# A hybrid SSD / MLA / stick-breaking trunk: sums and transfers around the FFN moved in the program, padded k_pe for the scores, one product of two k-tiles moved

## The chip, the cores and the metric

The kernel runs on one core of a Trainium2 chip. The metric is the device time of one execution in microseconds; lower is better. Times given for a kernel are the median of several runs, and beside them stands one execution under the hardware profiler, whose trace all readings of the profile use.

TensorE (PE in the profile) multiplies matrices, VectorE (DVE) and ScalarE (ACT) work elementwise, GpSimd (POOL) and SyncE (SP) here mostly issue transfers.

## The reference

A trunk of two pre-norm residual layers over 256 positions of width 2048, float32. Layer 0 runs a Mamba-2 mixer and latent attention (MLA) side by side behind one input projection and into one output projection. Layer 1 is stick-breaking attention. Each layer is followed by a SwiGLU FFN with a hidden width of 5632:

```python
def swiglu_ffn(h, w_gate, w_up, w_down):
    return (jax.nn.silu(h @ w_gate) * (h @ w_up)) @ w_down

# MLA, 16 heads, two query blocks of 128 (q_nope, k_nope: 128 wide; q_pe, k_pe: 64 wide, k_pe shared)
s = (jnp.einsum('bqhd,bkhd->bhqk', q_nope[:, q0:q1], k_nope[:, :q1])
     + jnp.einsum('bqhr,bkr->bhqk', q_pe[:, q0:q1], k_pe[:, :q1])).astype(jnp.float32) * scale

for layer in range(DEPTH):
    h = rms_norm(x, mix_norm[layer])
    ...
    x = x + mix
    x = x + swiglu_ffn(rms_norm(x, ffn_norm[layer]), w_gate[layer], w_up[layer], w_down[layer])
return rms_norm(x, final_norm)
```

## The kernel before

**Numbers.** Products are kept near float32 by splitting each operand into a high part (fp32r) and the rest. ScalarE casts the high part (`split`, L316), VectorE subtracts it (L322), and a product of one k-tile (128 rows of the contraction) is three matmuls: high by high, low by high, high by low. Activations are split once, each weight tile (128 x 4 k-tiles x 512, 1 MB) once as it is used.

**Weight tiles.** `weight_slots` lays out an arena: three slots for high parts (`wh`, a fourth from the first output projection on), six (`w`) into which SP loads raw tiles and in which the low part takes the raw tile's place, two (`wsum`) for sums of weight tiles. `wtile` gives out the free slot that was last used longest ago. The residual x lives in `xres`, behind the slots. During an FFN, from its second pair on, `lend` turns `xres` into one more `w` and one more `wsum` slot ("lent" in the profile); x waits in DRAM meanwhile (`saved`, four blocks of 512 columns, 512 KB each), where the partial results of the down projection are added by transfers. `load_residual` brings it back at the FFN's end.

**Pairs.** Two projections of the same operand (512 columns each, left and right) are one `pair`. For two groups of four k-tiles it uses seven products of a Strassen-like scheme (M1 to M7, 12 matmuls each) instead of eight, with four accumulators in PSUM (z, p3, p2, p4); some products need sums of weight tiles (t1, t2, M3's and M4's, `wsub`, L673), and accumulators that two results share are copied out in between (`kept`, L747, ScalarE). The order is written out as a list. In HALF the other eight k-tiles are four tiles c0 to c3 of plain products (24 matmuls each), 180 matmuls in all. In MORE the k-tiles 8 to 11 go through seven half-size products as well (n0, n1, n2, n3, six matmuls a product, with half-size sums t1 to t4), 174 in all. In "n0" the split tile serves M1 and then M2; "n2" serves M5 and then M6 from the sum T2. MORE needs sums of the activation blocks, made by `more_sums`; the FFN uses HALF for its first two pairs and MORE from the third (n >= 2).

**FFN.** Eleven pairs of gate and up, each giving 512 columns of h (`left` and `right`, L846 to L852). h is rounded by a transfer in SBUF that POOL issues (L855, the "h words") and transposed on TensorE (L327) in a task, `wait` ticks into the next work. Every second pair's h goes into four `down` projections (48 matmuls each), of which two follow each later pair; the last three chunks go into the final projections (72 matmuls each).

**Order.** TensorE's instructions run in the order of the text. Tasks (`spawn`) are generators that are advanced a step when the number of ticks that they yielded has gone by; there is a tick about every six matmuls. On the other engines a list scheduler orders the instructions by data and by rank (`priority`, `urgent`); `issue_after` puts an instruction behind another one on its engine. `s2` tiles come from a pool of 42.

**Start of an FFN.** While the second pair of the output projection before it runs, `norm_next` prepares the FFN's operand: blocks 0 and 1 through `norm_operand`, blocks 2 and 3 through `norm_block` (transposes, L329; split with the gain, L347 and L349; square sums, L312). Each writes its block of xres to `saved` (L536, L465). `more_sums` (L505 on) follows block 2.

**Scores.** `mla_head` adds three matmuls per query block into one tile: nope (L1417), rope (L1418, over 64 partitions: k_pe stands twice, in each half of `kpeT`, and a head uses the half in which its q_pe lies) and the mask (L1419, bf16).

Of the kernel before, what the change touches and what calls it, by code (L numbers as in the profile page):

```python
# [15 lines left out]
P = 128  # L16
# [24 lines left out]
class Trunk:  # L41
# [204 lines left out]
    def constant_tiles(self, rows_m, rows_a, rows_b):  # L246
        nc = self.nc
        c = lambda shape, name, dt=F32: self.cp.tile(shape, dt, name=name)
        self.ident = c([P, P], "ident")
        make_identity(nc, self.ident)  # L250
        warm = self.small([P, 1], "warm")
        nc.scalar.activation(warm, self.ident[:, 0:1], AF.Exp)
        self.ident_r = c([P, P], "ident_r", F32R)
        nc.gpsimd.dma_start(self.ident_r.bitcast(F32), self.ident)
        self.identb = c([P, P], "identb", BF16)
        make_identity(nc, self.identb)
        self.ones = c([P, P], "ones")
        nc.gpsimd.memset(self.ones, 1.0)

        self.tri_u = c([P, P], "tri_u")  # L260
        nc.gpsimd.affine_select(self.tri_u, self.ones, [[1, P]], ALU.is_ge, 0.0, base=0, channel_multiplier=-1)
        tri_l = self.s2([P])
        nc.gpsimd.affine_select(tri_l, self.ones, [[-1, P]], ALU.is_ge, 0.0, base=0, channel_multiplier=1)
        self.tri_l, self.ones_r = c([P, P], "tri_l", F32R), c([P, P], "ones_r", F32R)
        nc.gpsimd.tensor_copy(self.tri_l, tri_l)
        nc.gpsimd.tensor_copy(self.ones_r, self.ones)
        zero = self.s2([P])
        nc.gpsimd.memset(zero, 0.0)

        self.cmask = c([P, P], "cmask", BF16)  # L270
        nc.gpsimd.affine_select(self.cmask, zero, [[-1, P]], ALU.is_ge, NEG, base=0, channel_multiplier=1)

        self.vm, self.va, self.vb = c([P, 32], "vm"), c([P, 56], "va"), c([P, 120], "vb")
        self.g_mix = (self.vm[:, 0:16], self.vm[:, 16:32])
        self.g_ffn = (self.va[:, 0:16], self.va[:, 16:32])
# [55 lines left out]
    def transpose_split(self, src, res, g=None, wait=3, rank=None):  # L331

        for k2 in range(2):
            yield wait if k2 == 0 else 1
            pt = self.tr([2, S])
            for k in range(2):
                for t in range(2):
                    self.transpose(pt[:, k, t * P:(t + 1) * P], src(t, 2 * k2 + k))
            hi, lo = self.s2([2, S], F32R), self.s2([2, S], F32R)
            if g is None:  # L340
                with self.urgent() if rank == self.URGENT else self.priority(rank or self.tc.cur_priority):
                    self.split(hi, lo, pt)
            else:
                with self.urgent() if rank == self.URGENT else self.priority(rank or self.tc.cur_priority):
                    gk = [g[:, kk:kk + 1] for kk in (2 * k2, 2 * k2 + 1)]
                    for k in range(2):
                        act = self.nc.scalar.activation(hi[:, k], pt[:, k], AF.Copy, scale=gk[k])  # L347
                    for k in range(2):
                        dve = self.nc.vector.scalar_tensor_tensor(lo[:, k], pt[:, k], gk[k], hi[:, k].bitcast(F32),  # L349
                                                                  op0=ALU.mult, op1=ALU.subtract)  # L350
                if rank and rank >= 99000 and k2 == 0:
                    self.first = [act.ins, dve.ins]
            res.append((hi, lo))
# [101 lines left out]
    def norm_block(self, st, j, g, wait=2, rank=None, blocks=False, spill=None, pause=2):  # L455

        x, res = self.xres, []

        def gen():
            yield from self.transpose_split(  # L460
                lambda t, k: x[:, t, j * 512 + k * P:j * 512 + (k + 1) * P], res, g[:, 4 * j:4 * j + 4], wait, rank)
            for t in range(2):
                self.square_sum(x[:, t, j * 512:(j + 1) * 512], st["ssq"][:, t, j:j + 1])
            if spill is not None:
                self.nc.gpsimd.dma_start(spill[j], x[:, :, j * 512:(j + 1) * 512])  # L465
        st["xT"].append((self.spawn(gen()), res))
        if blocks and j == 1:
            self.make_sums(st, pause)
# [36 lines left out]
    def more_sums(self, st):  # L505

        sub = lambda o, p, q: self.nc.vector.tensor_tensor(o, p, q, op=ALU.subtract)
        add = lambda o, p, q: self.nc.vector.tensor_tensor(o, p, q, op=ALU.add)
        yield 1
        self.join(st["xT"][2][0])  # L510
        a = {}
        for j, (hi, lo) in enumerate(st["xT"][2][1]):
# [16 lines left out]
    def norm_operand(self, st, j, g):  # L529

        x = self.xres

        def squares():
            for t in range(2):
                self.square_sum(x[:, t, j * 512:(j + 1) * 512], st["ssq"][:, t, j:j + 1])
            self.nc.gpsimd.dma_start(self.saved[j], x[:, :, j * 512:(j + 1) * 512])  # L536
        self.operand_block(st, j, lambda t, k: x[:, t, j * 512 + k * P:j * 512 + (k + 1) * P],
                           g[:, 4 * j:4 * j + 4], squares, 9)

# [125 lines left out]
        w.left = uses  # L665
        return wh, wl, w

    def wsub(self, o, p, q, so=None, sp=None, sq=None):

        half = lambda w, n: w.raw if n is None else w.raw[:, 2 * n:2 * n + 2]  # L670
        with self.priority(self.wprio):
            self.wprio += 100
            ins = self.nc.vector.tensor_tensor(half(o, so), half(p, sp), half(q, sq), op=ALU.subtract).ins  # L673
        for w in (p, q):
            w.readers.append(ins)
        if not o.readers:
            self.filled(o, ins)
# [4 lines left out]

    MORE = ("M1", "M5", "c2", "t1", "t2", "t4", "n0", "n2", "M3", "M6", "M2", "t3", "M4", "n1", "M7", "n3", "c3")

    LATE = ("M1", "M5", "M3", "M6", "M2", "M7", "M4", "c0", "c1", "c2", "c3")

    def pair(self, st, va, vb, left, right, order=HALF):

# [79 lines left out]

        def halves(w, *ms):
            wh, wl, slot = w
            for n, (m, keep) in enumerate(ms):
                at = slice(2 * n, 2 * n + 2)
                add(bank[m], more_ops(m), (wh[:, at], wl[:, at], slot), keep and m)
        for m in order:
# [12 lines left out]
                self.wsub(src["n3"], raw["c0"], src["n2"], 0, 1, 1)  # L791
                continue
            if m == "n0":
                halves(self.wsplit(raw["c0"], 4, 4, mybir.DependencyClass.Sync), ("M1", True), ("M2", False))
                continue
            if m == "n2":
                halves(self.wsplit(src["n2"], 4, 4, mybir.DependencyClass.Sync), ("M5", True), ("M6", False))
# [11 lines left out]
            if m == "M5":  # L809
                self.wsub(t2, b22, t1)  # L810
            if m == "M3":
                self.wsub(b12, b22, b12)
            if m == "M6":
                load("b21")
                b21 = src["M2"] = raw["b21"]
# [6 lines left out]
            if m[0] == "c":  # L822
# [3 lines left out]
                    add(b, x[b in ("z", "p4")], w)  # L826
                continue
            add(bank[m], ops(m), w, m if m in keeps else None)

    def lend(self):  # L830

# [4 lines left out]
    def ffn(self, layer, st, gain_next):  # L836
# [308 lines left out]
    def dt_and_krope(self, rstd, xT):  # L1145
# [260 lines left out]
    def mla_head(self, h, qp, q, k, v, g, o, wait, done):  # L1406
# [6 lines left out]
        pr = slice(64 * (h % 2), 64 * (h % 2) + 64)  # L1413
        sc = self.at([3 * P])
        for q0, q1, c0, ks in ((0, P, 0, P), (P, S, P, S)):
            dst = sc[:, c0:c0 + ks]
            nc.tensor.matmul(dst, qT[:, q0:q1], kT[:, 0:ks], start=True, stop=False)  # L1417
            nc.tensor.matmul(dst, qpT[pr, q0:q1], self.kpeT[pr, 0:ks], start=False, stop=False)  # L1418
            nc.tensor.matmul(dst[:, ks - P:ks], self.identb, self.cmask, start=False, stop=True)  # L1419
        mx, sm = self.small([P, 2], "mx"), self.small([P, 2], "sm")  # L1420
        p = self.s2([3 * P])
# [74 lines left out]
```

## Time and profile before

| | |
|---|---|
| median of 3 runs | 2420.68 us (2420.16 to 2421.95) |
| profiled execution | 2423.95 us, span 2422.2 us, mean granted TensorE clock 0.996 |
| TensorE busy | 2382.6 us (98%), 10936 matmuls |
| VectorE busy | 2007.2 us (83%) |
| ScalarE busy | 1463.6 us (60%) |
| transfers | 497.88 MB, mean 206 GB/s |
| first MLA scores, last | 428.9 us, 560.9 us |
| first FFN pair of layer 0 | from about 634 us |
| steady FFN stretch of layer 0 | a pair and two downs every 62.4 us |

The span is the time from the first to the last instruction of the profiled execution; times below are from its start. Busy times of matmuls overlap, so the distance from one start to the next is the better measure of a product's cost.

### The profile page before, as it was taken

How to read it: one execution, taken by the hardware profiler on the slowest of the kernel's cores; microseconds unless marked ns; L12 is line 12 of the kernel's file. 1: busy time of each engine (PE TensorE's matmuls, PEld its weight loads, DVE VectorE, ACT ScalarE, POOL GpSimd, SP SyncE). 2: the span in 40 equal slices, each digit the busy share in tenths (PEclk: the TensorE clock that was granted, in tenths of full speed). 3: DMA queues.
4: the chain of work that ended last, by engine and by line, in shares of the span. 5: the costliest groups of instructions: out<-in, count | busy, mean ns of one | idle time of the engine just before them, and what ended most of it. 6: DMA issues, size and time to landing. Idle time of an engine off the chain costs nothing.

```text
span 2422.2 us, 28061 instructions
## 1 busy us (share of the span) xinstructions
PE 2382.6 (98%) x10936; PEld 1956.7 (81%) x10936; DVE 2007.2 (83%) x1664; ACT 1463.6 (60%) x1480; POOL 233.8 (10%) x301
## 2 busy tenths in 40 slices
PE   8999999999999999999999999999999999999998
PEld 7888888777778888888888888888778888888877
DVE  6776597578999888888887989779998888998874
ACT  6665465555755665656655686775655565666663
POOL 1342001120000000000010010000000000000011
PEclk9999999999999999999999999999999999999999
DMA  7655556434656777777776555556667777777773
GB/s 261 201 182 192 186 191 186 117 131 156 222 196 226 221 232 230 220 233 235 224 222 225 199 175 180 184 174 226 211 206 229 224 226 224 227 226 229 226 251 119
DMA packets 274902, 497.88 MB, mean 206 GB/s; under 512 B 22924, under 2 KB 48144, under 8 KB 274768
## 3 DMA queue, kind: packets, MB, share of 16 engines
q1 hardware_dynamic: 255440, 446.48, 55.7%
q0 software_dynamic: 18752, 48.55, 8.0%
q8 instruction: 86, 1.41, 0.2%
q10 hardware_dynamic: 576, 1.05, 0.1%
q14 instruction: 48, 0.39, 0.0%
HBM read 459.24 MB, written 25.20 MB: 200 GB/s over the span
## 4 chain that ended last, share of the span: by engine, by line
PE 73%; issue 13%; DVE 9%; DMA 2%; POOL 2%; ACT 1%; SPq 0%; POOLq 0%; DVEq 0%; ACTq 0%
PE acc L726 39%; PE acc L421 10%; PE acc L424 10%; PE acc L423 10%; DVE wsum L673 2%; DVE wsum L322 2%; DVE w L322 2%; DMA s<-s 1%; DVE lent L322 1%; DVE lent L673 1%; PE at L1341 1%; PE tr L327 1%; DVE w L673 0%; POOL s L1245 0%; DVE s L322 0%
## 5 line engine op out<-in xcount | busy, mean ns | idle before, releaser
L322 DVE TENSOR_TENSOR w<-w,wh 128x2048 fp32r<-128x2048 f32 (+2 forms) x397 | 885.8, 2242 | 199.4 <-ACT wh L316 189.4
L726 PE MATMUL acc<-wh,s 128*128 128x512 f32 x3888 | 991.6, 393 | 7.3 <-DVE s L322 3.1
L316 ACT CAST wh<-w 128x2048 fp32r<-128x2048 f32 (+2 forms) x397 | 741.6, 1874 | 350.1 <-PE acc L424 133.8
L726 PEld LDWEIGHTS acc<-wh,s 128*128 128x128 f32 x3888 | 727.4, 189 | 160.1 <-ACT s L747 4.3
L421 PE MATMUL acc<-wh,s 128*128 128x512 f32 (+1 forms) x1280 | 510.8, 399 | 2.0 <-ACT wh L316 2.0
L424 PE MATMUL acc<-wh,s 128*128 128x512 f32 (+1 forms) x1280 | 496.9, 388 | 0.0
L423 PE MATMUL acc<-w,s 128*128 128x512 f32 (+1 forms) x1200 | 464.9, 387 | 0.0
L726 PE MATMUL acc<-w,s 128*128 128x512 f32 x1304 | 355.7, 391 | 0.4 <-DVE w L322 0.4
L726 PEld LDWEIGHTS acc<-w,s 128*128 128x128 f32 x1304 | 245.7, 189 | 53.5 <-DVE w L322 1.8
L424 PEld LDWEIGHTS acc<-wh,s 128*128 128x128 f32 x1280 | 240.8, 188 | 50.3
L421 PEld LDWEIGHTS acc<-wh,s 128*128 128x128 f32 x1280 | 241.2, 188 | 48.0 <-ACT wh L316 2.4
L423 PEld LDWEIGHTS acc<-w,s 128*128 128x128 f32 x1200 | 226.3, 189 | 43.6 <-issue 1.4
L316 ACT CAST wh<-wsum 128x2048 fp32r<-128x2048 f32 x103 | 186.7, 1813 | 74.7 <-DVE wsum L673 53.3
L322 DVE TENSOR_TENSOR wsum<-wsum,wh 128x2048 fp32r<-128x2048 f32 x103 | 222.8, 2163 | 4.0 <-ACT wh L316 4.0
L316 ACT CAST wh<-lent 128x2048 fp32r<-128x2048 f32 (+1 forms) x66 | 120.5, 1836 | 75.4 <-DMA lent<-in_w_gate_dram 33.6
L322 DVE TENSOR_TENSOR lent<-lent,wh 128x2048 fp32r<-128x2048 f32 (+1 forms) x66 | 144.0, 2186 | 8.6 <-ACT wh L316 8.2
L673 DVE TENSOR_TENSOR wsum<-w,wsum 128x2048 f32<-128x2048 f32 (+1 forms) x52 | 106.1, 2041 | 25.0 <-PE acc L726 20.9
L726 PE MATMUL acc<-wsum,s 128*128 128x512 f32 x388 | 109.2, 396 | 5.9 <-DVE wsum L322 5.3
L747 ACT COPY s<-acc 128x512 f32<-128x512 f32 x132 | 77.0, 584 | 57.2 <-PE acc L726 57.0
L855 POOL DMA_DIRECT2D s<-s x44 | 24.5, 557 | 783.7 <-DVE s L852 733.9
L726 PEld LDWEIGHTS acc<-wsum,s 128*128 128x128 f32 x388 | 72.1, 189 | 26.3 <-DVE wsum L322 11.8
L871 POOL DMA_DIRECT2D saved<-s x64 | 56.5, 1026 | 331.1 <-ACT s L870 331.1
(262 smaller groups left out, 1868.6 us busy)
## 6 DMA issues: line engine op xcount, KB each, us to landing
w<-in_w_down_dram SPq DMA_DIRECT2D x78, 1024.0 KB, 5.0
w<-in_w_gate_dram SPq DMA_DIRECT2D x76, 1024.0 KB, 5.1
w<-in_w_up_dram SPq DMA_DIRECT2D x76, 1024.0 KB, 5.2
w<-in_w_qkv_dram SPq DMA_DIRECT2D x48, 1024.0 KB, 5.0
w<-in_w_in_dram SPq DMA_DIRECT2D x47, 1024.0 KB, 5.1
w<-in_w_out_even_dram SPq DMA_DIRECT2D x32, 1024.0 KB, 5.0
saved<-s POOLq DMA_DIRECT2D x64, 256.0 KB, 6.7
w<-in_w_out_odd_dram SPq DMA_DIRECT2D x16, 1024.0 KB, 4.9
```

Of the source, the lines that this page charges most:

```text
L316: cast = nc.scalar.copy(hi, src).ins
L322: return nc.vector.tensor_tensor(lo, src, hi.bitcast(F32), op=ALU.subtract).ins
L327: self.nc.tensor.transpose(out.bitcast(F32R), src, self.ident_r)
L421: nc.tensor.matmul(ps[t], hi[:, ts], wh, start=k == 0, stop=False)
L423: slot.used(nc.tensor.matmul(ps[t], hi[:, ts], wl, start=False, stop=False), self.clock)
L424: nc.tensor.matmul(ps[t], lo[:, ts], wh, start=False, stop=k == nk - 1)
L673: ins = self.nc.vector.tensor_tensor(half(o, so), half(p, sp), half(q, sq), op=ALU.subtract).ins
L726: m = nc.tensor.matmul(ps[b], x, y, start=b not in started, stop=stop, skip_group_check=True)
L747: self.kept = nc.scalar.copy(o, ps[b]).ins
L855: nc.gpsimd.dma_start(words.bitcast(F32), h[t])
L871: nc.gpsimd.dma_start(self.saved[n][:, t], s, accum_op=ALU.add)
L1341: nc.tensor.matmul(py[:, ds], rows[c, h // 4][:, h % 4], xdt[c][:, ds], start=True, stop=True)
```

## The change

- `more_sums` begins 40 ticks after it is spawned instead of one; MORE begins with the fourth pair (n >= 3).
- The four writes of xres to `saved` leave `norm_operand` and `norm_block` (as called ahead of an FFN) and become a task at the FFN's start, one each four ticks. It is joined before `lend`.
- The four reads of `saved` at the FFN's end become a task, the first after 12 ticks, then one each six.
- h's transposes wait ten ticks instead of six, except the last chunk's.
- In the first pair, M3's weight sum is queued on VectorE behind the low part of operand block 2.
- In MORE, the M2 part of n0 becomes an entry of its own, n4, behind n2.
- `kpeT` becomes two tiles of 128 partitions, each with k_pe in one half and zeros in the other; the rope product runs over 128 partitions. The tile of ones becomes a view of `ones_r`.

```diff
@@ constant_tiles
-        self.ones = c([P, P], "ones")
-        nc.gpsimd.memset(self.ones, 1.0)
+        ones = self.s2([P])
+        nc.gpsimd.memset(ones, 1.0)
...
-        nc.gpsimd.tensor_copy(self.ones_r, self.ones)
+        nc.gpsimd.tensor_copy(self.ones_r, ones)
+        self.ones = self.ones_r.bitcast(F32)
@@ transpose_split
+                self.lo = dve.ins
@@ norm_block
+            if j == 2:
+                st["lo"] = self.lo
@@ more_sums
-        yield 1
+        yield 40
         self.join(st["xT"][2][0])
@@ norm_operand
-            self.nc.gpsimd.dma_start(self.saved[j], x[:, :, j * 512:(j + 1) * 512])
@@ wsub
-        with self.priority(self.wprio):
+        with self.priority(self.wprio), self.tc.issue_after(after) if after else nullcontext():
@@
-    MORE = ("M1", "M5", "c2", "t1", "t2", "t4", "n0", "n2", "M3", "M6", "M2", "t3", "M4", "n1", "M7", "n3", "c3")
+    MORE = ("M1", "M5", "c2", "t1", "t2", "t4", "n0", "n2", "n4", "M3", "M6", "M2", "t3", "M4", "n1", "M7", "n3", "c3")
@@ pair
             if m == "n0":
-                halves(self.wsplit(raw["c0"], 4, 4, mybir.DependencyClass.Sync), ("M1", True), ("M2", False))
+                first = self.wsplit(raw["c0"], 4, 4, mybir.DependencyClass.Sync)
+                halves(first, ("M1", True))
+                continue
+            if m == "n4":
+                halves(first, None, ("M2", False))
                 continue
...
             if m == "M3":
-                self.wsub(b12, b22, b12)
+                self.wsub(b12, b22, b12, after=st["lo"] if after == "lo" else after)
@@
+    def residual_back(self):
+        for j in range(4):
+            yield 12 if j == 0 else 6
+            self.nc.gpsimd.dma_start(self.xres[:, :, j * 512:(j + 1) * 512], self.saved[j])
+
+    def residual_away(self):
+        for j in range(4):
+            yield 4
+            self.nc.gpsimd.dma_start(self.saved[j], self.xres[:, :, j * 512:(j + 1) * 512])
@@ ffn
-                      self.MORE if n >= 2 else self.HALF)
+                      self.MORE if n >= 3 else self.HALF, None if n else "lo")
...
-                lambda t, k, h=tuple(h): h[t][:, k * P:(k + 1) * P], res, wait=6, rank=self.URGENT)), res
+                lambda t, k, h=tuple(h): h[t][:, k * P:(k + 1) * P], res, wait=10 if n < HID // 512 - 1 else 6, rank=self.URGENT)), res
...
+        away = self.spawn(self.residual_away())
         for n in range(HID // 512):
             if n == 1:
+                self.join(away)
                 self.lend()
...
-        self.load_residual(lambda j: self.saved[j])
+        self.spawn(self.residual_back())
@@ norm_next
-            self.norm_block(st, n, g, 2 if n == 2 else 6, self.URGENT, spill=self.saved)
+            self.norm_block(st, n, g, 2 if n == 2 else 6, self.URGENT)
@@ dt_and_krope
+        self.kpeT = self.small([P, 2, S], "kpeT", bufs=1)
+        nc.vector.memset(self.kpeT, 0.0)
...
-        self.kpeT = self.small([P, S], "kpeT", bufs=1)
-        nc.vector.tensor_copy(self.kpeT, pk)
+        for a in range(2):
+            half = slice(64 * a, 64 * a + 64)
+            nc.vector.tensor_copy(self.kpeT[half, a], pk[half])
@@ mla_head
-            nc.tensor.matmul(dst, qpT[pr, q0:q1], self.kpeT[pr, 0:ks], start=False, stop=False)
+            nc.tensor.matmul(dst, qpT[:, q0:q1], self.kpeT[:, h % 2, 0:ks], start=False, stop=False)
```

More of the change, by code (lines that the diff above doesn't have):

```diff
@@ L256, in constant_tiles @@
         make_identity(nc, self.identb)
-        self.ones = c([P, P], "ones")
-        nc.gpsimd.memset(self.ones, 1.0)
+        ones = self.s2([P])
+        nc.gpsimd.memset(ones, 1.0)
         self.tri_u = c([P, P], "tri_u")
-        nc.gpsimd.affine_select(self.tri_u, self.ones, [[1, P]], ALU.is_ge, 0.0, base=0, channel_multiplier=-1)
+        nc.gpsimd.affine_select(self.tri_u, ones, [[1, P]], ALU.is_ge, 0.0, base=0, channel_multiplier=-1)
         tri_l = self.s2([P])
-        nc.gpsimd.affine_select(tri_l, self.ones, [[-1, P]], ALU.is_ge, 0.0, base=0, channel_multiplier=1)
+        nc.gpsimd.affine_select(tri_l, ones, [[-1, P]], ALU.is_ge, 0.0, base=0, channel_multiplier=1)
         self.tri_l, self.ones_r = c([P, P], "tri_l", F32R), c([P, P], "ones_r", F32R)
         nc.gpsimd.tensor_copy(self.tri_l, tri_l)
-        nc.gpsimd.tensor_copy(self.ones_r, self.ones)
+        nc.gpsimd.tensor_copy(self.ones_r, ones)
+        self.ones = self.ones_r.bitcast(F32)
         zero = self.s2([P])
@@ L666, in wsplit, with wsub @@
         return wh, wl, w
-    def wsub(self, o, p, q, so=None, sp=None, sq=None):
+    def wsub(self, o, p, q, so=None, sp=None, sq=None, after=None):
         half = lambda w, n: w.raw if n is None else w.raw[:, 2 * n:2 * n + 2]
-        with self.priority(self.wprio):
+        with self.priority(self.wprio), self.tc.issue_after(after) if after else nullcontext():
             self.wprio += 100
@@ L681, with pair @@
     HALF = ("M1", "M5", "c0", "M3", "M6", "M2", "M4", "M7", "c2", "c1", "c3")
-    MORE = ("M1", "M5", "c2", "t1", "t2", "t4", "n0", "n2", "M3", "M6", "M2", "t3", "M4", "n1", "M7", "n3", "c3")
+    MORE = ("M1", "M5", "c2", "t1", "t2", "t4", "n0", "n2", "n4", "M3", "M6", "M2", "t3", "M4", "n1", "M7", "n3", "c3")
     LATE = ("M1", "M5", "M3", "M6", "M2", "M7", "M4", "c0", "c1", "c2", "c3")
-    def pair(self, st, va, vb, left, right, order=HALF):
+    def pair(self, st, va, vb, left, right, order=HALF, after=None):
         nc = self.nc
@@ L774, in halves @@
             wh, wl, slot = w
-            for n, (m, keep) in enumerate(ms):
+            for n, part in enumerate(ms):
+                if part is None:
+                    continue
+                m, keep = part
                 at = slice(2 * n, 2 * n + 2)
@@ L793, in pair @@
             if m == "n0":
-                halves(self.wsplit(raw["c0"], 4, 4, mybir.DependencyClass.Sync), ("M1", True), ("M2", False))
+                first = self.wsplit(raw["c0"], 4, 4, mybir.DependencyClass.Sync)
+                halves(first, ("M1", True))
+                continue
+            if m == "n4":
+                halves(first, None, ("M2", False))
                 continue
@@ L1412, in mla_head @@
         qpT, qT, kT = qp[1][0][:, h // 2], q[1][h // 2][:, h % 2], k[1][h // 2][:, h % 2]
-        pr = slice(64 * (h % 2), 64 * (h % 2) + 64)
         sc = self.at([3 * P])
```

## The prediction

> **What bounds the kernel now.** I read the shares of busy time first, then the busy time by stretch, then TensorE's timeline for the places where its products come late, then the engine that each late place waits for.
>
> ```profile
> PE 2382.6 (98%) x10936; PEld 1956.7 (81%) x10936; DVE 2007.2 (83%) x1664; ACT 1463.6 (60%) x1480; POOL 233.8 (10%) x301
> ...
> 416.00:575.00 159.00, 157.38 (x817) 124.29 (x816) 109.28 (x163) 88.19 (x168) 23.21 (x37) 1.00 0.41 126
> 695.00:747.00 52.00, 51.44 (x232) 42.16 (x230) 47.30 (x30) 29.37 (x23) 1.07 (x2) 1.00 0.64 213
> ```
>
> TensorE is busy for 2382.6 us of 2422.2, so a change pays only where it shortens TensorE's stream or closes a place where TensorE is late. The last two lines are stretches (length, then busy PE, PEld, DVE, ACT, POOL, granted clock, DMA share and GB/s): in the MLA stretch TensorE is busy 157.38 of 159 us and VectorE 109.28, so time taken out of TensorE's stream there is taken out of the kernel. Each edit below has its own place, read from a timeline (start, length, engine, line, shapes, count, idle before).
>
> **1. k_pe beside zeros (16 heads).** One head's scores, and further down products of the same sizes over all 128 rows:
>
> ```profile
> 428.88 0.38 PE L1417 MATMUL at<-s,s 128*128 128x128 f32 x2
> 429.20 0.48 PE L1418 MATMUL at<-kpeT,s 64*128 64x128 f32 x2
> 429.61 0.23 PE L1419 MATMUL at<-cmask,identb 128*128 128x128 bf16 x1
> 429.68 0.65 PE L1417 MATMUL at<-s,s 128*128 128x256 f32 x2
> 430.26 0.70 PE L1418 MATMUL at<-kpeT,s 64*128 64x256 f32 x2
> 430.89 0.23 PE L1419 MATMUL at<-cmask,identb 128*128 128x128 bf16 x1
> ...
> 450.34 0.59 PE L1441 MATMUL at<-s,s 128*128 128x256 f32 x2
> 450.77 0.38 PE L1442 MATMUL at<-s,s 128*128 128x128 f32 x2
> 450.99 0.49 PE L1435 MATMUL tr<-ident,s 128*128 128x128 f32 x3
> ```
>
> Start to start, a 128-row pair over 256 columns takes 0.43 us (450.34 to 450.77) and over 128 columns 0.22. In the head, the 64-row pairs take 0.63 (430.26 to 430.89) and 0.41, and the 128-row pairs just ahead of them 0.58 and 0.32: both sides of the change of height pay. From 428.88 to 430.89 is 2.01 us. With all rows 128 high I count 0.22 + 0.22 + 0.07 + 0.43 + 0.43, and leave 0.06 for the product behind the short bf16 mask product, whose weights have only 0.07 us to load in: 1.43. That is 0.58 a head, **-9.3 us** for 16. Bounds: only what the 64-row pairs themselves lose, 0.19 + 0.20, gives -6.2; with the 0.06 too, -10.3; and 0 if another engine held the stretch, which the 157.38 speaks against. Zeros add no product: the count of matmuls stays. The memset and the second half copy (0.4 us each at most, by VectorE's 128x256 rows below) run on a VectorE that is free a third of the time. The tile of ones becomes a view of ones_r: nothing.
>
> The Trainium skill, "TensorEngine Tiling (Array Packing)", Tiling Modes, Key Properties, says that changing the tiling mode drains TensorE; the trace's 0.58 beside 0.43 ahead of the switch agrees. The same page, When to Use Tiling, recommends 2x row tiling where the contraction is 64, which speaks against padding to 128: by it the padded form could give up to half of those pairs' time away, +0.32 a head instead of -0.58. It needs two products in different row halves side by side, and here each head's pair stands alone between 128-row products; no row shows an overlap, and I go by the rows.
>
> **2. More sums later (yield 40), start of each FFN.** The first FFN pair's M6:
>
> ```profile
> 647.77 1.97 PE L726 MATMUL acc<-wh,s 128*128 128x512 f32 x8
> 652.38 1.20 PE L726 MATMUL acc<-wsum,s 128*128 128x512 f32 x4 [2.63 <-DVE wsum L322]
> 653.41 3.51 PE L726 MATMUL acc<-wh,s 128*128 128x512 f32 x8
> ...
> 1731.99 1.96 PE L726 MATMUL acc<-wsum,s 128*128 128x512 f32 x4 [2.63 <-DVE wsum L322]
> ...
> 635.52 1.26 DVE L349 SCALAR_TENSOR_TENSOR s<-tr,va,s 128x256 fp32r<-128x256 f32 x3
> 636.70 1.28 DVE L508 TENSOR_TENSOR s<-s,s 128x512 f32<-128x512 f32 x2
> 637.90 2.28 DVE L322 TENSOR_TENSOR w<-w,wh 128x2048 fp32r<-128x2048 f32 x1
> 640.10 0.42 DVE L508 TENSOR_TENSOR s<-s,s 128x256 f32<-128x256 f32 x1
> 641.11 2.28 DVE L673 TENSOR_TENSOR w<-w,w 128x2048 f32<-128x2048 f32 x1
> ...
> 647.05 2.28 DVE L673 TENSOR_TENSOR wsum<-w,wsum 128x2048 f32<-128x2048 f32 x1
> 650.04 2.28 DVE L322 TENSOR_TENSOR wsum<-wsum,wh 128x2048 fp32r<-128x2048 f32 x1
> ```
>
> Eight products take 1.81 us from start to start at full rate (0.227 each), so M6's low products were due at 649.58 and came at 652.38: 2.80 late. Then they run slow for a while: eight in 3.51 instead of 1.97, and about 0.1 at either side. Together 4.4 us, and the same in layer 1 (2.63 idle, 1.96 instead of 1.07 at once): 8.8. The wait is for VectorE, which works without a pause and still has the more sums ahead of this split: 636.70 to 637.90, 640.10 to 641.11, and between 641.11 and 647.05 whatever is not the sum and a split of 2.20 each: 1.20 + 1.01 + 1.54 = 3.75 us. Without them the split of 650.04 ends about 648.5, a microsecond ahead of need. **-8.8**; at worst the wait comes back where the sums go (below).
>
> Does a later place in the text move them? Two rows say when it does:
>
> ```profile
> 623.67 0.69 POOL L465 DMA_DIRECT2D saved<-xres  x1 [31.56 <-DVE xres L558]
> 635.09 0.65 ACT L312 ACTIVATE s<-xres 128x512 f32<-128x512 f32 x1
> ```
>
> Both read the same block of xres and stand behind its transposes in the text. The transfer, which takes no tile of the pool, left as soon as the data were there; the square sum, which takes an s2 tile, went 11 us later behind the splits. So the more sums, which take s2 tiles, should follow their place. They land in the second pair, where VectorE has 52.00 - 47.30 = 4.7 us free for 3.75, and are needed only by the fourth pair.
>
> By the same rows the spaced spills (residual_away) and reloads (residual_back) should go when they went before: **0**. Their cover, if they move instead: four spills in the first pair, 2 MB at the 213 GB/s of the stretch above, are 10 us of transfers in 41 us of products with DMA at 0.64; and reloads behind the last h words could close a wait like those of part 3 at each last pair, up to -3.5. POOL has nothing else queued there than the h words; the lent slots' first load on SP would wait for the last spill, with a pair's time in hand. M3's sum behind block 2's low part is already in that order (641.11 behind 635.52): 0.
>
> **3. h's transposes four ticks later.**
>
> ```profile
> 686.79 1.07 PE L726 MATMUL acc<-w,s 128*128 128x512 f32 x4
> 689.59 0.51 PE L327 MATMUL tr<-ident_r,s 128*128 128x128 f32 x4 [1.73 <-DMA s<-s]
> 691.29 2.04 PE L726 MATMUL acc<-wh,s 128*128 128x512 f32 x4
> ...
> 733.49 0.51 PE L327 MATMUL tr<-ident_r,s 128*128 128x128 f32 x4 [0.56 <-DMA s<-s]
> 1769.41 0.59 PE L327 MATMUL tr<-ident_r,s 128*128 128x128 f32 x4 [1.97 <-DMA s<-s]
> 1813.62 0.51 PE L327 MATMUL tr<-ident_r,s 128*128 128x128 f32 x4 [0.90 <-DMA s<-s]
> ```
>
> Four ticks are 24 products, 5.4 us: more than any of these waits. Beside the idle 1.73 the transposes start 0.16 later still (689.59 against 687.70 due), and the next eight products lose about 1.5 more at the slow rate (2.04 where 1.07 is usual, and the four after it in part). So 3.4 + 0.7 + 3.4 + 1.1 = **-8.6**. Nobody is late for it: the transposed chunk is read only behind the next pair, and the last one keeps its 6.
>
> The slow products behind 2 and 3 are some 1.5 us in each of four places, 6 in all. The Trainium skill, "TensorE: Matmul & The Clock Gate", Part 1, has TensorE fall to half clock after an idle window of about 3.4 us that runs freely. Here 1.7 to 2.6 us of idling were followed by it, so the row decides that a stall of that size costs the slow products too.
>
> **4. M2 of tiles 8 to 11 behind T2's products (n4).** A pair in the steady stretch:
>
> ```profile
> 865.37 0.62 PE L726 MATMUL acc<-wsum,s 128*128 128x512 f32 x2
> 869.90 1.98 PE L726 MATMUL acc<-wh,s 128*128 128x512 f32 x8
> 871.93 1.20 PE L726 MATMUL acc<-wsum,s 128*128 128x512 f32 x4
> ...
> 861.02 2.29 DVE L322 TENSOR_TENSOR wsum<-wsum,wh 128x2048 fp32r<-128x2048 f32 x1
> 867.38 2.29 DVE L673 TENSOR_TENSOR wsum<-w,wsum 128x2048 f32<-128x2048 f32 x1 [1.88 <-PE acc L726]
> 864.21 1.91 ACT L316 CAST wh<-w 128x2048 fp32r<-128x2048 f32 x1 [0.27 <-PE acc L726]
> 866.03 0.58 ACT L747 COPY s<-acc 128x512 f32<-128x512 f32 x1
> ...
> 742.66 2.29 DVE lent L673
> 2321.96 2.29 DVE wsum L673
> ```
>
> The low part of M6 comes 2.03 us behind its high part instead of 1.81, and is drawn out (1.20 for 1.07): 0.35 a pair, taken as 0.33. The chain of waits has it 18 times, the first at 742.66 and the last at 2321.96. M4's sum (867.38) waits for the slot of T2's sum, which TensorE has just read. With T2's products six earlier (1.36 us) it starts 1.36 earlier, and the wait is gone: 18 x 0.33 = **-5.9**, bounds 0 and that. The new need: T2's low part at 865.37 - 1.36 = 864.01; it is there at 863.31.
>
> **5. The third pair in the order HALF.** MORE has 174 products, HALF 180: six more of 0.227, in two layers: **+2.7**. Its two half sums and a split and a half less only relieve VectorE.
>
> **Sum.** -9.3 - 8.8 - 8.6 - 5.9 + 2.7 = -29.9. The profiled execution took 2423.95 us (span 2422.2), which would become 2394.0; it is 3.3 above the median of 2420.68, so I forecast 2420.7 - 29.9 = **2391**.
>
> **Rivals.**
> - *The sums stay, or stall the second pair instead.* VectorE's 4.7 us free against 3.75 is thin. Then 8.8 is not gained: 2400. For it: VectorE is busy almost throughout; against: nothing needs them for two pairs.
> - *Heads no faster*, because the row tiling was worth what it cost, or because the transposes that wait for POOL's rotation or VectorE's maxima come up against their inputs: 9.3 lost, 2400. Against: TensorE idles 1.6 us in 159. With the one above: 2409.
> - *The slow products stay.* If, as the clock gate's rule has it, a free window and not these stalls sets them, they fall elsewhere: 6 lost, 2397.
> - *Slower.* ScalarE issues in order. Its cast at 864.21 waits for the high tile of the first half product, which M2 now holds 2.7 us longer, to about 866.9. If M5's copy (866.03) stays behind that cast, it ends at 866.9 + 1.9 + 0.6 = 869.4, and M3, which needs the bank at 867.2, is 2.2 late in each of 16 pairs: 35 us, with slow products at 1.5 each up to 59. That gives 2426 to 2450; the change loses by more than 0.2% from 2.2 us a pair. Against: the copy is ready at 864.6 and has the higher rank.
> - *No change*: the gains come back as other waits of VectorE or DMA: 2418.
>
> **How the numbers follow.** My forecast 0.48, sums 0.20, heads 0.12, both 0.04, slow products 0.07, slower 0.05, no change 0.04. The range runs from 2384 (heads at -10.3, reloads at -3.5, and 2 of scatter) to 2409, which leaves out 0.09 of the cases. Measurement can tell about 0.2% (4.8 us) from no change: faster 0.91, same 0.04, slower 0.05.
>
> **What would show it.** Right: no 64-row form, a head's scores in 1.43 us; M6 of each first pair without a 2.63 wait and its eight products in 1.97; no wait for the h words at the second and third pair; 0.22 gone from M6 in the steady pairs; 180 products in the third pair. Wrong: a wait for VectorE in the second to fourth pair, or M3 waiting for ScalarE in every pair.

## The result and the profile after

The changed kernel takes **2384.68 us** (median of 4 runs, 2384.23 to 2386.92); the kernel before, run beside it, 2420.42 (4 runs, 2418.32 to 2421.95). The ratio is 0.9852, with a 95% interval of 0.9838 to 0.9866: 35.7 us gone, where 29.9 were forecast (2391, range 2384 to 2409). The profiled execution took 2384.55 us, span 2382.8.

Shares of busy time, then the MLA stretch and the second FFN pair (length, then busy PE, PEld, DVE, ACT, POOL, granted clock, DMA share, GB/s), after:

```profile
PE 2359.7 (99%) x10948; PEld 1956.2 (82%) x10948; DVE 1995.9 (84%) x1654; ACT 1460.3 (61%) x1476; POOL 234.9 (10%) x301
...
416.00:563.00 147.00, 146.32 (x811) 124.82 (x810) 107.93 (x163) 87.16 (x167) 20.95 (x36) 1.00 0.43 133
661.00:702.00 41.00, 41.00 (x187) 33.95 (x186) 40.48 (x32) 25.54 (x22) 1.09 (x2) 1.00 0.66 218
```

Twelve matmuls more (the two third pairs) and 23 us less busy TensorE: the scores' products became quicker, and the slow products went. VectorE fills the second pair to 40.48 of 41.00, and TensorE has no gap there.

What TensorE waited for, in total, times and longest: first of before, then of after.

```profile
PE tr L327 <- DMA s<-s: 8.5, 6, 2.0
PE acc L726 <- DVE wsum L322: 5.3, 2, 2.6
...
```

```profile
...
PE acc L729 <- DVE wsum L323: 0.2, 1, 0.2
...
```

The six waits for the h words (transposes, L327, now L328) are gone, the two for M6's sum have shrunk to one of 0.25 us, and nothing new of size stands in their place. "Six" matters: four of them lie at the second and third pairs, two at the last pairs, and the forecast had four in its sum and only a bound for the other two.

Where the time went, from the starts and ends of the pairs in both profiled executions:

| place | before to after, us |
|---|---|
| kernel start to the first pair of the mixer | -1.8 |
| from there to the second out-projection pair (MLA heads in it) | -12.2 |
| first FFN pair, layer 0 and 1 (its own length) | -4.61, -4.57 |
| second | -3.47, -3.67 |
| third (six products more) | +0.23, -0.11 |
| fourth to eleventh, 16 pairs | -0.37 to -0.40 in 13, -0.77 and -0.67 in two, -0.07 in the last: -6.6 |
| behind the last pair (wait for the h words) | -1.86, -1.62 |
| mixer and output projection of layer 1 | +0.5 |

The start, the mixer of layer 1, and some 2.6 of the 12.2 differ by about as much between traces of kernels that are the same in that place (the start by 1.7 us among those made from the changed kernel); they are not put down to the change. Some 1.6 of the 2.6 are slow products behind a stall of 2.4 us; the stall came in both executions, the slow products only in before's.

Slow products are stretches at half clock. In before, the granted clock is 0.50 for 3.41 us each, from 578.44, 653.53, 691.08, 1732.14 and 1769.69 us; in after it falls for the first time 6 us ahead of the span's end (the record begins some 11 to 15 us into the span). Two of the five lie in the first pairs of the two FFNs and two in the second pairs.

**Heads.** TensorE's timeline of a head, after:

```profile
427.11 0.39 PE L1442 MATMUL at<-s,s 128*128 128x128 f32 x2
427.33 0.39 PE L1443 MATMUL at<-kpeT,s 128*128 128x128 f32 x2
427.56 0.22 PE L1444 MATMUL at<-cmask,identb 128*128 128x128 bf16 x1
427.61 0.65 PE L1442 MATMUL at<-s,s 128*128 128x256 f32 x2
428.10 0.59 PE L1443 MATMUL at<-kpeT,s 128*128 128x256 f32 x2
428.53 0.22 PE L1444 MATMUL at<-cmask,identb 128*128 128x128 bf16 x1
428.56 0.36 PE L423 MATMUL acc<-wh,s 128*128 128x256 f32 x1
```

427.11 to 428.53 is 1.42 us, for 2.01. Up to the start of the product behind the mask it is 1.45 for 2.05 (to 0.02) in each of the 16 heads, 9.6 us in all.

**M6 of the first pair**, layer 0 and layer 1, and VectorE ahead of it in layer 0:

```profile
633.57 1.98 PE L729 MATMUL acc<-wh,s 128*128 128x512 f32 x8
635.41 1.20 PE L729 MATMUL acc<-wsum,s 128*128 128x512 f32 x4
636.45 2.00 PE L729 MATMUL acc<-wh,s 128*128 128x512 f32 x8
...
1702.50 1.19 PE L729 MATMUL acc<-wsum,s 128*128 128x512 f32 x4 [0.25 <-DVE wsum L323]
...
633.07 2.28 DVE L323 TENSOR_TENSOR wsum<-wsum,wh 128x2048 fp32r<-128x2048 f32 x1
...
668.10 1.28 DVE L512 TENSOR_TENSOR s<-s,s 128x512 f32<-128x512 f32 x2
...
678.57 0.41 DVE L511 TENSOR_TENSOR s<-s,s 128x256 f32<-128x256 f32 x1
```

The eight products take 2.00 again. The split ends at 635.35 and TensorE needs it at 635.38: where the forecast had a microsecond in hand there is nothing; in layer 1 it is 0.25 short. The more sums run from 668 to 679, inside the second pair.

**h's transposes**, second pair, without a wait, and a steady pair, with ScalarE's rows in it:

```profile
675.85 0.46 PE L328 MATMUL tr<-ident_r,s 128*128 128x128 f32 x4
...
847.74 1.98 PE L729 MATMUL acc<-wh,s 128*128 128x512 f32 x8
849.56 1.07 PE L729 MATMUL acc<-lent,s 128*128 128x512 f32 x4
...
842.50 0.59 ACT L750 COPY s<-acc 128x512 f32<-128x512 f32 x1 [0.77 <-PE acc L729]
844.77 1.92 ACT L317 CAST wh<-w 128x2048 fp32r<-128x2048 f32 x1 [1.68 <-PE acc L729]
```

M6's low part follows its high part by 1.82 us (before 2.03) and takes 1.07 (before 1.20). ScalarE's copy for M5 (842.50) went ahead of the cast that waits for M2, so the slower rival did not come.

### The profile page after: what moved, and what is told of

It is laid out like the page before. It is cut to its first block, busy times and chain, and to the rows that moved or that the text cites. A ratio compares the mean times of both kernels' runs of the same rounds, so it can differ in the third digit from the quotient of the medians.

```text
span 2382.8 us, 28019 instructions
## 1 busy us (share of the span) xinstructions
PE 2359.7 (99%) x10948; PEld 1956.2 (82%) x10948; DVE 1995.9 (84%) x1654; ACT 1460.3 (61%) x1476; POOL 234.9 (10%) x301
## 4 chain that ended last, share of the span: by engine, by line
PE 90%; issue 5%; ACT 1%; DMA 1%; DVE 1%; POOL 0%; SPq 0%; POOLq 0%; DVEq 0%; ACTq 0%
PE acc L729 51%; PE acc L423 11%; PE acc L426 11%; PE acc L425 11%; ACT wh L317 1%; PE at L1367 1%; PE tr L328 1%; PE tr L364 1%; PE at L1442 0%; DMA w<-in_w_in_dram 0%; PE at L1443 0%; PE tr L330 0%; DVE w L323 0%; POOL spare L1067 0%; DMA w<-in_w_out_even_dram 0%
## 5 line engine op out<-in xcount | busy, mean ns | idle before, releaser
L425 PE MATMUL acc<-w,s 128*128 128x512 f32 (+1 forms) x1216 | 471.0, 387 | 0.3 <-DVE w L323 0.3
L323 DVE TENSOR_TENSOR wsum<-wsum,wh 128x2048 fp32r<-128x2048 f32 (+1 forms) x101 | 218.4, 2162 | 6.3 <-ACT wh L317 6.3
L317 ACT CAST wh<-wsum 128x2048 fp32r<-128x2048 f32 (+1 forms) x101 | 182.8, 1810 | 45.6 <-PE acc L729 25.3
L317 ACT CAST wh<-lent 128x2048 fp32r<-128x2048 f32 (+1 forms) x62 | 114.5, 1857 | 63.2 <-DMA lent<-in_w_gate_dram 27.4
L323 DVE TENSOR_TENSOR lent<-lent,wh 128x2048 fp32r<-128x2048 f32 (+1 forms) x62 | 137.1, 2217 | 12.5 <-ACT wh L317 12.3
```

Of the source, the lines that this page charges most:

```text
L317: cast = nc.scalar.copy(hi, src).ins
L323: return nc.vector.tensor_tensor(lo, src, hi.bitcast(F32), op=ALU.subtract).ins
L425: slot.used(nc.tensor.matmul(ps[t], hi[:, ts], wl, start=False, stop=False), self.clock)
```

## The experiments

Theory: the five terms of the forecast are separate, and the 3.5 us at the last pairs come from the turn of the lent slots. Each kernel below takes one piece away or does it alone. Those that start from the changed kernel are set against its ratio of 0.9852. Differences in us are of medians, against 2384.68 for kernels made from the changed one; by the ratios, which go by the kernel before as it ran beside each, they come out up to 1.8 us otherwise, so anything smaller is read from the traces alone.

**k_pe alone**, in the kernel before:

```diff
+        self.kpeT = self.small([P, 2, S], "kpeT", bufs=1)   # zeros, k_pe in one half each
-            nc.tensor.matmul(dst, qpT[pr, q0:q1], self.kpeT[pr, 0:ks], start=False, stop=False)
+            nc.tensor.matmul(dst, qpT[:, q0:q1], self.kpeT[:, h % 2, 0:ks], start=False, stop=False)
```

> The kernel before with the padded k_pe (and the view for the tile of ones) alone. If the scores' loss came from the 64-row products and TensorE bounds the MLA stretch, this alone takes 9.3 to 10.4 us off (about 2410), the distance from a head's first score product to its second mask product falls from 2.01 to 1.43 us, and nothing else moves. Rival: the stretch is bound elsewhere or the rope products gain little: under 4 us off, with new TensorE waits for GpSimd's rotation or VectorE's maxima between 420 and 560 us.

2410.5 (5 runs), ratio 0.9966 (0.9953 to 0.9979): -10.0 by the medians, -8.2 by the ratio; its 16 heads take 9.6 us less than before's, head for head the same as in the changed kernel, and no FFN pair changes by more than 0.4. Behind the last pair of layer 1 its profiled execution is 2.8 longer than before's, where the wait for the h words was 3.0 this time.

**What the 64-row products pay for.** The kernel before, with each head's products in the order nope, nope, rope, rope, mask, mask. This order also alters what is summed in the scores; the number and shapes of the products are the same.

```diff
-        for q0, q1, c0, ks in ((0, P, 0, P), (P, S, P, S)):   # nope, rope, mask of one block
+        for ... in blocks: nope
+        for ... in blocks: rope   # 64 rows, one behind the other
+        for ... in blocks: mask
```

> The kernel before, with the products of a head's scores in another order: both 128-row pairs, then both 64-row pairs, then both mask products; k_pe stays 64 rows high, no other part of the change. Switching theory (each step from 128 to 64 rows and back costs about 0.1 us, and there are now two steps in a head, not four): about half of the 0.6 us a head goes, -5 against before, 2415.5. Weight-load theory (each 64-row product pays for its own weight load, wherever it stands): the four 64-row products of a head lose what they lost, at most one step less, -1.6, 2419.

2416.5 (10 runs), ratio 0.9981 (0.9971 to 0.9992): -5.6 by the medians, -4.6 by the ratio. The head in it:

```profile
429.46 0.82 PE L1417 MATMUL at<-s,s 128*128 128x128 f32 x4
430.21 0.92 PE L1420 MATMUL at<-kpeT,s 64*128 64x128 f32 x4
431.06 0.28 PE L1424 MATMUL at<-cmask,identb 128*128 128x128 bf16 x2
431.15 0.36 PE L421 MATMUL acc<-wh,s 128*128 128x256 f32 x1
```

429.46 to 431.15 is 1.69 us, between before's 2.05 and after's 1.45: one visit to 64 rows instead of two, and 0.35 of the 0.60 gone (5.6 in 16 heads). Instruction by instruction, the first 64-row product comes 0.31 behind the last 128x256 of the nope pair (0.22 without a change of height), the second 0.21 behind the first (0.11 is usual), the third and fourth at 0.11 and 0.22, which is the full rate, and the mask 0.31 behind the last (0.22). So a 64-row product inside a run of them costs nothing extra; it is the way in and out that does, some 0.3 us a visit. The weight-load theory falls.

**More sums early again** (in the changed kernel):

```diff
-        yield 40
+        yield 1
```

> The changed kernel with the more sums after one tick again (all else as changed). If the later sums are what frees the first FFN pair, its M6 waits for VectorE again: 2.6 us idle and slow products behind it in each layer, 4.4 us a layer, together about 8.8 us longer than the changed kernel (2393 to 2394). Rival: the moved spills or M3's place behind the low part freed it, then the time stays within 1 us of 2384.7. With M3's sum behind block 2 the wait could also be shorter than before: 4 to 9 us is still the theory.

2395.07, ratio 0.9897 (0.9882 to 0.9912): +10.4. The first pairs are 4.57 and 4.58 us longer, with the wait and the slow products of before:

```profile
639.87 1.20 PE L729 MATMUL acc<-wsum,s 128*128 128x512 f32 x4 [2.65 <-DVE wsum L323]
640.90 3.29 PE L729 MATMUL acc<-wh,s 128*128 128x512 f32 x8
```

The other FFN pairs keep their lengths; the rest of the +10.4 lies in places that vary from one execution to the next.

**M3's sum without its order** (in the changed kernel):

```diff
-                      ..., None if n else "lo")
+                      ..., None)
```

> The changed kernel without the order that puts M3's sum of the first pair behind block 2's low part; all else of the change stays. Theory (the sum came behind that low part already in the kernel before): 0 against the changed kernel, 2384 to 2386, the first pair of each FFN 42.6 and 43.0 us long. Rival (the order holds the sum off VectorE's stream until the splits are through): M6 of the first pair waits for VectorE by up to one sum of 2.28 us in each layer, 2387 to 2390.

2388.08, ratio 0.9861 (0.9845 to 0.9878): +3.4 by the medians, +2.2 by the ratio, within the intervals no difference; the trace is plain. The first pairs are 1.17 and 1.19 us longer, for a wait that neither kernel had:

```profile
627.49 0.96 PE L729 MATMUL acc<-wh,s 128*128 128x512 f32 x3 [1.06 <-DVE s L350]
...
624.75 2.29 DVE L676 TENSOR_TENSOR w<-w,w 128x2048 f32<-128x2048 f32 x1
626.95 0.88 DVE L350 SCALAR_TENSOR_TENSOR s<-tr,va,s 128x256 fp32r<-128x256 f32 x2
```

A sum of 2.29 us now stands ahead of the second half of the low parts. The order is worth 2.4 us in that trace. In the kernel before, the sum came behind the low part without it; probably the moved sums changed the list around it, but no run here separates them from the other edits.

**h's transposes at six ticks again** (in the changed kernel):

```diff
-    wait=10 if n < HID // 512 - 1 else 6
+    wait=6
```

> The changed kernel with h's transposes six ticks behind for every chunk. If the four extra ticks are the cause, TensorE waits for the h words at the second pair (about 3.4 us a layer with the slow products) and a little at the third (0.7 to 1.1): 7 to 9 us longer than the changed kernel, 2392 to 2394. Rival: the words land sooner now for another reason (fewer transfers beside them), then the loss is under 3 us.

2394.01, ratio 0.9895 (0.9881 to 0.991): +9.3. The second and third pairs are longer by 2.25, 2.28, 1.62 and 3.57; one wait of 0.89 lies between two pairs. Two of the four, with what follows them:

```profile
670.97 0.50 PE L328 MATMUL tr<-ident_r,s 128*128 128x128 f32 x4 [2.07 <-DMA s<-s]
671.31 1.16 PE L729 MATMUL acc<-wh,s 128*128 128x512 f32 x4
...
1786.03 0.58 PE L328 MATMUL tr<-ident_r,s 128*128 128x128 f32 x4 [1.86 <-DMA s<-s]
1786.40 2.04 PE L729 MATMUL acc<-wh,s 128*128 128x512 f32 x4
```

The longer stall is followed by products at the full rate, the shorter one by slow ones.

**M2 back in n0** (in the changed kernel):

```diff
-    MORE = (..., "n0", "n2", "n4", ...)   # n0: M1; n4: M2
+    MORE = (..., "n0", "n2", ...)         # n0: M1, M2
```

> The changed kernel with M2's half product back in n0, ahead of T2's. If n4 closes M6's wait, each pair from the fourth on is 0.35 to 0.40 us longer again (39.6 us instead of 39.2 from first to last product), 16 pairs, 5.6 to 6.4 us: about 2391. Rival for the last pair's wait: if n4 also changed which slot is lent last, the reloads of x move back beside the last h words and another 1.8 us a layer comes on top, about 2394.

2391.38, ratio 0.9886 (0.9869 to 0.9902): +6.7; 15 pairs are 0.35 longer each, 5.3 us together:

```profile
849.35 1.98 PE L729 MATMUL acc<-wh,s 128*128 128x512 f32 x8
851.38 1.19 PE L729 MATMUL acc<-lent,s 128*128 128x512 f32 x4
```

2.03 and 1.19 again. The last pairs' wait for the h words stays away, so n4 is not its cause.

**Spills and reloads in their old places** (in the changed kernel):

```diff
-        away = self.spawn(self.residual_away())
-        self.spawn(self.residual_back())
+        # spills in norm_operand and norm_block
+        self.load_residual(lambda j: self.saved[j])
```

> The changed kernel with the spills of xres issued in the norm and the reloads issued all at once behind the down pass, as before the change; all else of the change stays. Theory (a transfer that takes no pool tile leaves when its data and its slot are ready, wherever its task stands; the reloads went 20 us ahead of the last h words because the lent slots come free earlier, through the order HALF in the third pair): 0 against the changed kernel, 2384 to 2386, reloads again near 1223 us, no wait for the h words at the last pair of either FFN. Rival (spacing the reloads keeps them out of the h words' way): the last pair's wait for the h words is back, 1.8 us in each layer, 2388.

2385.47, ratio 0.9857 (0.9842 to 0.9871): no difference. POOL's queue at the last pair, in this kernel, then in the changed one, then in the kernel before:

```profile
1223.24 2.89 POOL L556 DMA_DIRECT2D xres<-saved  x4 [16.65 <-PE acc L730]
1243.08 1.21 POOL L876 DMA_DIRECT2D s<-s  x2 [16.95 <-DVE s L873]
```

```profile
1222.83 2.88 POOL L843 DMA_DIRECT2D xres<-saved  x4 [16.21 <-PE acc L729]
1242.66 1.21 POOL L875 DMA_DIRECT2D s<-s  x2 [16.95 <-DVE s L872]
```

```profile
1265.67 2.18 POOL L552 DMA_DIRECT2D xres<-saved  x3 [33.62 <-PE acc L726]
1268.51 1.22 POOL L855 DMA_DIRECT2D s<-s  x2 [0.65 <-DVE s L852]
1269.71 0.71 POOL L552 DMA_DIRECT2D xres<-saved  x1
```

With or without the spaced tasks the reloads leave 20 us ahead of the last h words, released by TensorE's last product from the lent slots. Before, they left 3 us ahead, and the h words landed in their midst. From issue to landing (size, median us), after and then before:

```profile
s<-s POOLq DMA_DIRECT2D x2, 256.0 KB, 3.2
```

```profile
s<-s POOLq DMA_DIRECT2D x2, 256.0 KB, 5.9
```

**The third pair's order**, from both sides: HALF there alone in the kernel before, and MORE there in the changed kernel.

```diff
-                      self.MORE if n >= 2 else self.HALF)
+                      self.MORE if n >= 3 else self.HALF)   # and the reverse
```

> The kernel before, with the order HALF in the third pair of each FFN (180 products for 174), no other part of the change. Theory (the turn of the lent slots is set by the third pair's order): 12 products more cost +2.7, and the lent slots are read about 40 us earlier at the end, so the reloads leave ahead of the last h words and the last pair's wait of 1.8 us in each layer goes, -3.6; together -0.9, 2419.6. Rival (the third pair's order has no say in it): +2.7, 2423.2, the wait still there.

> The changed kernel with the order MORE from the third pair on (174 products) in place of HALF (180); all else of the change stays. Theory (the turn of the lent slots is set by the third pair's order): 12 products fewer give -2.7, but the lent slots are read about 40 us later again at the end, the reloads leave beside the last h words, and the last pair waits 1.8 us in each layer: +3.6; together +0.9, 2385.6. Rival (the spaced reloads, or n4, moved them): -2.7, 2382, without that wait. Second rival (the sums that now land in the second pair are not there when MORE needs them in the third): a wait for VectorE at the third pair of 2 to 4 us in each layer, 2386 to 2391.

HALF alone: 2419.09, ratio 0.9992 (0.9982 to 1.0001), no difference to be measured, and the two sides of it in the trace: the stretch from the third pair's start to the fourth's is 1.8 and 1.2 us longer, and the stretches behind the last pairs are 1.86 us shorter each, the wait gone. POOL's queue:

```profile
1244.27 2.89 POOL L552 DMA_DIRECT2D xres<-saved  x4 [15.89 <-PE acc L726]
1264.82 1.21 POOL L855 DMA_DIRECT2D s<-s  x2 [17.66 <-DVE s L852]
```

The reloads are 20 us ahead, with nothing else of the change there. MORE in the changed kernel: 2391.48, ratio 0.9881 (0.9864 to 0.9899), slower by 6.8 where 0.9 was expected. Its trace has something of the theory and of both rivals in it:

```profile
1241.09 1.48 POOL L843 DMA_DIRECT2D xres<-saved  x2 [33.62 <-PE acc L729]
1243.24 1.20 POOL L875 DMA_DIRECT2D s<-s  x2 [0.68 <-DVE s L872]
...
715.33 0.73 PE L729 MATMUL acc<-w,s 128*128 128x512 f32 x2 [0.67 <-DVE w L323]
717.53 0.73 PE L729 MATMUL acc<-lent,s 128*128 128x512 f32 x2 [0.54 <-DVE lent L323]
...
2317.74 0.51 PE L328 MATMUL tr<-ident_r,s 128*128 128x128 f32 x4 [1.73 <-DMA s<-s]
```

The reloads stand beside the h words again; in layer 0, where only two of the spaced ones are ahead of them, the h words come in time, in layer 1 TensorE waits 1.73 us and the slow products follow, 3.4 together. And the third pairs wait 0.67 and 0.54 for splits, so that with six products fewer they take 0.4 longer. That makes 4.2; its profiled span is 3.7 longer. The rest of the 6.8 is not in that execution.

**MORE there, with the sums earlier:**

```diff
-                      self.MORE if n >= 3 else self.HALF, ...)
+                      self.MORE if n >= 2 else self.HALF, ...)
-        yield 40
+        yield 26
```

> The changed kernel with the order MORE from the third pair on and the more sums at yield 26 in place of 40. Theory (in the run with MORE and yield 40 the third pair's splits came 0.67 and 0.54 late because the sums stood right ahead of them on VectorE): the 1.5 us lost in each third pair go, the third pair gains its 1.36 in each layer against the changed kernel, -2.7; the second layer's last pair still waits for its h words, +3.5; together 2385 to 2386. Rival (MORE itself needs more of VectorE at that place): the lateness stays, 2389 to 2391.

2388.66, ratio 0.9862 (0.9847 to 0.9877). The waits in the third pair are the same to the hundredth (0.67 and 0.54), though the more sums ran over 10 us earlier: the theory falls. What is left is MORE itself, which has five weight sums on VectorE just ahead of that split (between 702.13 and 713.08 us in the trace with yield 40). The last pair of layer 1 waits 2.69. No version tried is quicker than the changed kernel.

## Why the prediction was nearly right

The direction, the places and most of the mechanisms held; the size was 6 us short. Of these, 3.5 are the last pairs', and four other terms were short by 0.3 to 1.1 each.

| step | forecast | shown |
|---|---|---|
| 1 heads | -9.3 | -9.6 (16 heads, trace; -10.0 when done alone) |
| 2 more sums, first pairs | -8.8 | -9.2 |
| 3 and 5 second and third pairs | -5.9 (-8.6 + 2.7) | -7.0 |
| 4 n4 | -5.9 | -6.6 in the trace, 0.7 of it one-off (undone: 5.3 lost in the trace, 6.7 by the medians) |
| reloads and the last pairs | 0 (bound -3.5) | -3.5 |
| sum | -29.9 | -35.9; the medians differ by 35.7 |

- **The step that failed is the zero for the reloads.** Its reason held, that a transfer without a pool tile goes when its data are there: the spills left within 2 us of where they left before, measured from the FFN's first product, and undoing the spacing of spills and reloads changes nothing. What I did not follow is that the reloads' "data are there" hangs on the lent slots, and that step 5 changes their turn. Step 5 was costed by its products alone (+2.7, as measured: +3.0 when done alone) and gave back 3.7 at the other end of the FFN. The bound of -3.5 had the right place and size under the wrong cause, and it is what brought the result into the range: that was luck.
- **Heads.** 1.45 for 2.05 against a forecast of 1.43 for 2.01, between other marks. The 64 rows pay on the way in and out, as assumed. By the rule on 2x row tiling of the Trainium skill ("TensorEngine Tiling (Array Packing)", When to Use Tiling), as the forecast weighed it, they would have lost 0.32 each; the trace has a gain of 0.60.
- **Sums.** They moved, because of the pool tile, and the second pair's VectorE had room, with half a microsecond to spare (40.48 of 41.00). But the microsecond of reserve ahead of M6's split was not there, and "M3's order: 0" was wrong: without it the first pairs lose 2.4 to a wait for block 2's low parts that the forecast had not seen. Without the order the first pairs gained 6.8, where 8.8 was forecast for the sums; the order, forecast at 0, gave the other 2.4. That the two together came out at 9.2 is luck in part.
- **h's transposes.** All four waits went, and with them more than the 8.6: about 9.7 if the third pair's products are taken at 2.7.
- **n4.** Right mechanism; 15 pairs at 0.39, and in two of them 0.3 more that one late product of before had cost, for 18 at 0.33. The 18 was a slip: by the forecast's own step 5 the third pairs have no n4, which leaves 16.
- **Slow products.** They went with the stalls, as forecast; that rival (2397) fell. But the forecast's step from a stall's size to slow products does not hold: the 2.07 us stall above was followed by none, and nor, in before itself, were the 1.66 and 1.68 us stalls at the last pairs. The last section has what decides.
- The base: the profiled execution of before was 3.5 above its median, and 3.4 of what it took more than the profiled execution of after lie at the start and in slow products that both kernels can have. Summing against it and then subtracting from the median was the right care.

## What to carry to other kernels

When an edit changes how often buffers are used, follow each buffer's turn to its last user and see what that user releases, on other queues too: here an order of products in the third pair set when transfers could leave eight pairs later. A transfer's place in the text can say little: here the event that freed its data or its destination set when it left. And an ordering hint that is idle in the old schedule has to be costed in the new one.

## What was not expected of the hardware

- The cost of a lower contraction lies in changing the height of the products, about 0.3 us a visit (0.09 and 0.10 on the way in, 0.09 on the way out, in the grouped run), and not in the low products themselves, which run at 0.11 and 0.22 us like those of 128 rows.
- Stalls of TensorE between 1.7 and 2.9 us were followed by products at about half rate (2.04 us for four, where 1.16 is usual) in some cases and by none in others: after 1.73 and 1.86 (above), not after 2.07, nor after this one of the changed kernel:

```profile
566.10 0.50 PE L729 MATMUL acc<-wh,s 128*128 128x512 f32 x1 [2.36 <-DVE s L323]
566.43 1.09 PE L729 MATMUL acc<-w,s 128*128 128x512 f32 x4
```

  Where they came they cost 1.1 to 1.7 us. Two stretches of 3.41 us, the first in before behind the 1.73, the second in after from the end of that stall of 2.36 (columns as above; the clock is third from the end):

```profile
691.08:694.49 3.41, 3.41 (x13) 2.74 (x11) 2.71 (x3) 1.67 (x2) 0.00 (x0) 0.50 0.00 0
```

```profile
566.10:569.50 3.40, 3.40 (x15) 2.83 (x16) 3.37 (x3) 0.08 (x1) 0.00 (x0) 1.00 0.00 0
```

  The starts of the five stretches of before lie whole multiples of 3.413 us apart (22, 11, 305 and 11). With that grid laid over all twelve traces, from 30 us on, it is the idle time inside one window of 3.413 us that decides, and not the length of the stall: behind a window with 1.73 us or more of TensorE idle (by the ends that the profile gives its products) the next was at half clock in 28 of 30 cases (not after 1.76 in the run with six ticks and 1.88 in the grouped one), behind one with 1.71 or less in none. The stall of 2.41 us in before had 2.31 in one window; the one of 2.36 in after had 1.71. The Trainium skill, "TensorE: Matmul & The Clock Gate", Part 1, has the clock fall after an idle window of about 3.4 us, in windows that run freely. The window and its free running agree with these rows; an idle of the window's whole length was not needed, as about half was enough.
- The h words of layer 0's last pair, 256 KB each, landed in 3.2 us with weight loads but no reloads beside them (DMA share 0.99 from 1243 to 1246) and in 5.9 beside four reloads of 512 KB. Reloads are not the only thing that slows them: at the second and third pairs of before they took 5.4 to 5.9 with no reload near, in its steady pairs of layer 0 2.3 to 2.9.
